# Hybrid decoder trunk: which 32-byte place the split weight tiles start at

## The chip, the cores and the metric

The kernel runs on one core of a Trainium2 chip. The metric is device time in microseconds (us). Two timed runs of the kernel before the change took 1570.54 and 1565.43 us; their median is 1567.99 us.

The engines named below are TensorE (PE in the profile, with PEld for its weight loads), VectorE (DVE), ScalarE (ACT), GpSimd (POOL) and SyncE (SP), which issues the transfers.

## The reference, cut to what matters

Two layers (`DEPTH = 2`) work on 256 tokens of width 1024. Each layer is a half-step SwiGLU feed-forward block, a mixer with a Mamba-2 and a gated DeltaNet branch, and a second feed-forward block:

```python
for l in range(DEPTH):
    h = h + 0.5 * swiglu(rms_norm(h, ffn1_norm[l]), ffn1_w_in[l], ffn1_w_out[l])
    u = rms_norm(h, mix_norm[l])
    (z_s, xbc, dt_s, qkv, z_d, b_d, a_d, gate_s, gate_d) = jnp.split(u @ w_in[l], split_points, axis=-1)
    y_s = mamba2_branch(...)
    y_d = deltanet_branch(...)
    merged = (jax.nn.sigmoid(gate_s) * (y_s @ ssm_w_branch[l])
              + jax.nn.sigmoid(gate_d) * (y_d @ dn_w_branch[l]))
    h = h + merged @ w_out[l]
    h = h + 0.5 * swiglu(rms_norm(h, ffn2_norm[l]), ffn2_w_in[l], ffn2_w_out[l])
return rms_norm(h, final_norm)
```

`swiglu(x, w_in, w_out)` is `(silu(gate) * up) @ w_out` with `gate, up = split(x @ w_in)`; its inner width is 2816. All data are float32. Nearly all of the arithmetic is in products of activations with weights that are read from memory once.

## The kernel before, in words

**Split weights.** A float32 product is made from float32r matmuls. A weight tile of 128 partitions x 1024 columns is split in two: `hi`, the float32r rounding of the weights, made by an ACT copy (the helper `act`, L66), and `lo`, the rest, made by a DVE subtraction (the helper `tt`, L69). Activations are split in the same way (`uT`, `gh` and `gl`, `bh` and `bl`, `mh` and `ml`), and a product is the sum of hi x hi, hi x lo and lo x hi.

**The stream of weights.** `plan` lists the 552 split tiles in the order of their use, and `stream` the transfers that they need. `load` issues a transfer of 512 KB on SP's queue into one of five `wraw` buffers (or, for the first tile of a group in the feed-forward blocks, into `wfirst`, which shares buffers with `yz`). `prep` makes `whi` and `wlo`, in five buffers each (`NSPL = 5`). `take` hands the next split tile to the matmuls, after running `load` and `prep` ahead for the tiles that follow. A few tiles (kinds `q0` to `q6`) are combined with others by DVE before or after they are split, for a Strassen-like scheme with fewer products in the second half of the feed-forward blocks.

**Who uses a split tile.** With the letters of the change (matmuls counted from the loops):

- `f` (16 tiles, 192 matmuls) and `t` (64 tiles, 768): `tok_chunk`, L287 to L289, tiles `f` and `t` of the profile. The weights are streamed, 512 columns a matmul; `uT` is the operand loaded beforehand (the stationary one).
- `c` (160 tiles): `chan_pair`, tile `fc`. Weights are loaded and `uT` is streamed: 1280 matmuls of 512 columns (L342, with `hi`) alternate with 1280 of 256 columns (L346, with `lo`).
- `h` (112 tiles, 2688 matmuls of 256 columns): `chan_chunk`, L292 to L294, tiles `kk`, `qq`, `vv`, `bc`, `zd` and `xs`, with weights loaded and `uT` streamed.
- `p` and `o` (112 and 24 tiles, 672 and 288 matmuls): the products with the feed-forward block's second matrix, in `block_products` and `out_chunks`. Weights are streamed, `gh`, `gl` or the block sums `bsa` to `bsd` are loaded.
- `b` (48 tiles, 576 matmuls) and `w` (16 tiles, 192): the mixer's branch products and its output product, in `out_chunks`. Weights are streamed, `bh` and `bl`, or `mh` and `ml`, are loaded.

That is 7936 matmuls in all.

**Order of the work.** The order is written out by hand: `FFN` is the order inside a feed-forward block, `ORDER` that of the mixer's units. Matmuls wait for their weights by semaphores; `issue_after` and `high_priority` place a few ACT and DVE steps.

**Addresses.** Tiles lie one behind the other in each partition, in the order of the pools `cpool`, `wpool`, `slots`, `s2`, `sm`; each starts at a multiple of 32 bytes. The text calls the start address modulo 128 bytes, divided by 32, the *place* of a tile, 0 to 3. In the program before, the addresses are: `h` 16512, `uT` 32928, `wraw` from 57984, `whi` from 78464, `wlo` from 98944, `slots` from 119424 (`gh` 123520, `gl` 148096, `bsa` 172672, `bsb` 178816), `s2` from 203392. A whole tile of weights is 4096 bytes = 32 x 128, so all ten split buffers start at place 0, as do `gh`, `gl`, the block sums, `bh`, `bl`, `mh` and `ml`. Alone among the matmul operands of split products, `uT` starts at place 1, because `mhalf` (4 bytes, rounded up to 32) lies ahead of it. Every slice that a matmul takes of these tiles begins a multiple of 512 bytes into the tile, and so has the tile's place.

Of the kernel before, what the change touches and what calls it, by code (L numbers as in the profile page):

```python
# [8 lines left out]
F32R = mybir.dt.float32r  # L9
I32 = mybir.dt.int32  # L10
AF = mybir.ActivationFunctionType
ALU = mybir.AluOpType
# [4 lines left out]
P = 128  # L17
D = 1024
S = 256
DEPTH = 2  # L20
# [9 lines left out]
NRAW = 5  # L30
NSPL = 5
START = 2

FFN = "f" + 8 * "c" + "A" + 4 * "c" + "A" + 4 * "c" + "A" + 2 * "c" + "A" + 2 * "c" + "BdBBBddddd"
# [7 lines left out]
ORDER = """  # L44
# [7 lines left out]
def trunk_kernel(ctx, tc, x, wst, wsm, norms, lpar, rpar, cst, out):  # L52
    nc = tc.nc
    V, A, G, PE = nc.vector, nc.scalar, nc.gpsimd, nc.tensor

    cpool = ctx.enter_context(tc.tile_pool(name="cpool", bufs=1))
    wpool = ctx.enter_context(tc.tile_pool(name="wpool", bufs=1))
# [7 lines left out]
    def act(o, i, func=AF.Copy, **kw):  # L65
        return A.activation(out=o, in_=i, func=func, **kw)  # L66

    def tt(o, a, b, op):
        return V.tensor_tensor(out=o, in0=a, in1=b, op=op)  # L69
# [9 lines left out]
    def f(ap):  # L79
        return ap.bitcast(F32)  # L80

    def tmp2(name):
        return s2.tile([P, 512], F32, tag="s2", name=name)
# [52 lines left out]
    n_forms = len(plan)  # L136
# [3 lines left out]
    def load(j):  # L140
# [5 lines left out]
        state["last"] = nc.sync.dma_start(r[:], wst[stream[j] // 2, :, (stream[j] % 2) * 1024 :][:, 0:1024])  # L146
        raws[j] = r

    def prep(i):
        kind, js, _ = plan[i]  # L150
        hi = wpool.tile([P, 1024], F32R, tag="whi", name="whi", bufs=NSPL)
        lo = wpool.tile([P, 1024], F32R, tag="wlo", name="wlo", bufs=NSPL)

        def less(o, a, b):
            tt(raws[js[o]][:], raws[js[a]][:], raws[js[b]][:], ALU.subtract)


        r = raws[js[{"q2": 1, "q4": 4, "q5": 3}.get(kind, 0)]]
        with ExitStack() as behind:
            for ins in state["behind"].pop(i, ()):  # L160
                behind.enter_context(tc.issue_after(ins))
            act(hi[:], r[:])
            if kind == "q1":
                less(1, 2, 1)
            elif kind == "q2":
                less(0, 2, 0)
            elif kind == "q4":
                less(0, 3, 0)
            tt(lo[:], r[:], f(hi[:]), ALU.subtract)
            if kind == "q0":  # L170
                less(0, 1, 0)
        for o in {"d": (0,), "q2": (1,), "q3": (2,), "q4": (4,), "q5": (3,), "q6": (0,)}.get(kind, ()):
            raws.pop(js[o])
        halves[i] = (hi, lo)

    def ahead(key, n, fn):
        while state[key] < n:
            fn(state[key])
            state[key] += 1

    def take():
        j = state["taken"]
        state["taken"] = j + 1
        ahead("loaded", min(plan[min(j + NSPL, n_forms) - 1][2] + NRAW - 1, n_raw), load)
        ahead("prepped", min(j + 1 if state["hold"] else j + NSPL, n_forms), prep)
        return halves.pop(j)
# [11 lines left out]
    h = cpool.tile([P, 2, D], F32, name="h")  # L198
# [34 lines left out]
    def rstd_of(t):  # L233

        ss = small([P, 2], "ss")
        for n in range(2):
            junk = tmp2("junk")
            state["square"] = act(junk[:], h[:, t, n * 512 : (n + 1) * 512], AF.Square, scale=1.0 / 32.0, accum_out=ss[:, n : n + 1])
        z = small([P, 2], "zz")
        ts(z[:, 0:1], ss[:, 0:1], ss[:, 1:2], ALU.add, EPS, ALU.add)  # L240
        rsqrt(z[:, 1:2], z[:, 0:1], [P, 1])
        return z[:, 1:2]
# [18 lines left out]
    def norm_in(nw, add=None):  # L261

        for t in range(2):
            with tc.high_priority(offset=PRI), ExitStack() as behind:
                if add:
                    add(t)
                    if t == 0:
                        behind.enter_context(tc.issue_after(state["sums"][5].ins))
                ins, done = rms_chain(t, nw)
            if t == 0:  # L270
                state["hold"] = False
                n = state["taken"]
                if not add:
                    ahead("prepped", n + 1, prep)
                    with tc.issue_after(done[0].ins), tc.issue_after(done[1].ins):
                        ahead("prepped", n + START, prep)
                with tc.issue_after(ins.ins):
                    ahead("prepped", n + 2, prep)
                if add:
                    state["behind"][n + 2] = [d.ins for d in done]  # L280
            elif add:

                state["behind"][n + 4] = (state["square"].ins, ins.ins)
                state["input"] = done
# [946 lines left out]
    for t in range(2):  # L1231
        add(t)
        o = [tmp2("fo") for _ in range(2)]
# [3 lines left out]
        r = rstd_of(t)  # L1237
# [137 lines left out]
```

## Time and profile before

| | before |
|---|---|
| timed runs | 1565.43 and 1570.54 us, median 1567.99 us |
| span of the profiled execution | 1565.8 us (no other time of it is recorded) |
| TensorE busy | 1545.0 us, 10152 matmuls |
| weight loads busy | 1342.0 us |
| DVE, ACT busy | 1302.4 us, 999.8 us |
| `fc` on L342, 512 columns | 1280, mean 391 ns |
| `fc` on L346, 256 columns | 1280, mean 282 ns |
| granted TensorE clock | 0.999 |

How to read it: a matmul's duration runs from its start to the end of its last result, and matmuls overlap, so the duration of 391 ns is not what a matmul costs. What it costs is the step from its start to the start of the next one, which the timeline shows. Where a group's mean duration is longer than that of another group of the same shape, its steps are as a rule longer too.

### The profile page before, as it was taken

Reading aid. Unit: us, or ns where it says so; the run is one execution under the profiler, and the core shown is the slowest. Engines: PE = TensorE matmul, PEld = TensorE weight load, DVE = VectorE, ACT = ScalarE, POOL = GpSimd, SP = SyncE. Lnnn points to the kernel's source line nnn. Section 1 sums busy time; section 2 is a strip of 40 time slices with the busy share of each in tenths; the row PEclk is TensorE's granted clock in tenths of the full one; section 3 lists DMA queues with packets and bytes.
Section 4 is the critical chain, followed back from the end, with each engine's and each line's share of the span. In section 5 each row is a group of like instructions: output and inputs, shape, how many; then the busy total and the mean of one; then the engine's idle time right before and its main releaser. Section 6 shows DMA issues by size and latency. Waiting matters only on the chain.

```text
span 1565.8 us, 26672 instructions
## 1 busy us (share of the span) xinstructions
PE 1545.0 (99%) x10152; PEld 1342.0 (86%) x10152; DVE 1302.4 (83%) x2048; ACT 999.8 (64%) x1694; POOL 53.2 (3%) x60
## 2 busy tenths in 40 slices
PE   8999999999999999999999999999999999999998
PEld 6888779999888888888788887899998888888886
DVE  6889969957899766899878998699579996679897
ACT  6666668766675655666566676686656666466664
POOL 0000010000000000000000001010000000000000
PEclk9999999999999999999999999999999999999999
DMA  8565565553455555465765566555336546555553
GB/s 298 197 214 188 195 212 173 178 158 118 174 207 173 177 205 196 159 210 177 262 204 187 168 198 223 189 189 189 116 123 213 177 166 212 201 175 166 198 189 134
DMA packets 94215, 292.99 MB, mean 187 GB/s; under 512 B 22325, under 2 KB 23301, under 8 KB 93062
## 3 DMA queue, kind: packets, MB, share of 16 engines
q1 hardware_dynamic: 94086, 291.29, 55.2%
q8 instruction: 79, 1.29, 0.3%
q14 instruction: 50, 0.41, 0.1%
HBM read 289.33 MB, written 1.92 MB: 186 GB/s over the span
## 4 chain that ended last, share of the span: by engine, by line
PE 76%; DVE 13%; DMA 5%; issue 3%; ACT 2%; POOL 1%; SPq 0%; POOLq 0%; DVEq 0%; ACTq 0%
PE fc L342 15%; PE fc L346 8%; DVE wlo L69 7%; PE t L287 3%; PE t L288 3%; PE t L289 3%; DMA wraw<-in_wst_dram 3%; PE b L289 3%; PE b L288 3%; PE b L287 2%; PE xs L292 2%; PE xs L293 2%; PE xs L294 2%; PE o L288 1%; PE o L289 1%
## 5 line engine op out<-in xcount | busy, mean ns | idle before, releaser
L69 DVE TENSOR_TENSOR wlo<-wraw,whi 128x1024 fp32r<-128x1024 f32 x488 | 591.0, 1221 | 139.8 <-ACT whi L66 136.1
L66 ACT ACTIVATE whi<-wraw 128x1024 fp32r<-128x1024 f32 x488 | 511.6, 1057 | 176.4 <-PE b L289 29.8
L342 PE MATMUL fc<-uT,whi 128*128 128x512 f32 x1280 | 445.5, 391 | 0.0
L346 PE MATMUL fc<-uT,wlo 128*128 128x256 f32 x1280 | 360.9, 282 | 0.0
L342 PEld LDWEIGHTS fc<-uT,whi 128*128 128x128 f32 x1280 | 240.3, 188 | 50.7
L346 PEld LDWEIGHTS fc<-uT,wlo 128*128 128x128 f32 x1280 | 241.8, 189 | 0.8
L287 PE MATMUL t<-whi,uT 128*128 128x512 f32 x256 | 102.9, 403 | 0.0
L288 PE MATMUL t<-wlo,uT 128*128 128x512 f32 x256 | 101.5, 396 | 0.2 <-DVE wlo L69 0.2
L289 PE MATMUL t<-whi,uT 128*128 128x512 f32 x256 | 101.5, 397 | 0.0
L66 ACT ACTIVATE whi<-wfirst 128x1024 fp32r<-128x1024 f32 x64 | 67.8, 1059 | 29.7 <-DVE wfirst L69 20.4
L66 ACT ACTIVATE sg<-fc 128x256 f32<-128x256 f32 x80 | 30.6, 382 | 82.3 <-PE fc L346 82.3
L69 DVE TENSOR_TENSOR wlo<-wfirst,whi 128x1024 fp32r<-128x1024 f32 x64 | 78.1, 1220 | 2.0 <-ACT whi L66 1.9
L287 PE MATMUL b<-whi,bh 128*128 128x512 f32 x192 | 76.1, 398 | 0.0
L288 PE MATMUL b<-wlo,bh 128*128 128x512 f32 x192 | 74.9, 390 | 0.0
L289 PE MATMUL b<-whi,bl 128*128 128x512 f32 x192 | 74.3, 394 | 0.3 <-DVE bl L69 0.3
L292 PE MATMUL xs<-uT,whi 128*128 128x256 f32 x256 | 73.1, 286 | 0.0
L294 PE MATMUL xs<-uT,wlo 128*128 128x256 f32 x256 | 71.6, 280 | 0.0
L293 PE MATMUL xs<-uT,whi 128*128 128x256 f32 x256 | 71.4, 279 | 0.0
L288 PE MATMUL o<-wlo,gh 128*128 128x512 f32 x160 | 64.6, 404 | 2.6 <-DVE wlo L69 2.5
L69 DVE TENSOR_TENSOR wfirst<-wraw,wfirst 128x1024 f32<-128x1024 f32 x48 | 58.6, 1220 | 8.9 <-DMA wraw<-in_wst_dram 8.9
L289 PE MATMUL o<-whi,gl 128*128 128x512 f32 x160 | 62.5, 391 | 0.0
L287 PE MATMUL o<-whi,gh 128*128 128x512 f32 x160 | 62.1, 392 | 0.0
(317 smaller groups left out, 3424.5 us busy)
## 6 DMA issues: line engine op xcount, KB each, us to landing
wraw<-in_wst_dram SPq DMA_DIRECT2D x504, 512.0 KB, 4.5
wfirst<-in_wst_dram SPq DMA_DIRECT2D x16, 512.0 KB, 5.8
dc<-rdram SPq DMA_DIRECT2D x8, 1024.0 KB, 8.4
nw<-in_norms_dram SPq DMA_DIRECT2D x6, 512.0 KB, 6.2
gb<-rdram SPq DMA_DIRECT2D x8, 256.0 KB, 5.3
h<-in_x_dram SPq DMA_DIRECT2D x4, 256.0 KB, 5.7
out_dram<-fo SPq DMA_DIRECT2D x4, 256.0 KB, 2.1
dq<-X SPq DMA_DIRECT2D x2, 256.0 KB, 5.0
```

What stands on the lines that cost most here:

```text
L66: return A.activation(out=o, in_=i, func=func, **kw)
L69: return V.tensor_tensor(out=o, in0=a, in1=b, op=op)
L287: PE.matmul(ps, lh, rh, start=start, stop=False)
L288: PE.matmul(ps, lh, rl, start=False, stop=False)
L289: return PE.matmul(ps, ll, rh, start=False, stop=stop)
L292: PE.matmul(ps, wh, mh, start=start, stop=False)
L293: PE.matmul(ps, wh, ml, start=False, stop=False)
L294: PE.matmul(ps, wl, mh, start=False, stop=stop)
L342: PE.matmul(ps[a][:], wh[:, c0 : c0 + P], uT[:, kt].rearrange("p o t -> p (o t)"), start=kt == 0, stop=False,)
L346: PE.matmul(ps[a][:, 0:S], wl[:, c0 : c0 + P], uTh[:, kt, :], start=False, stop=kt == KT - 1)
```

## The change

Each split buffer becomes 24 columns (96 bytes) longer, 1048 columns in place of 1024, so that the five buffers of a kind start at five addresses that step by 96 modulo 128. A tile then uses 1024 of these columns from an offset `skip` that puts its start at a chosen place. `BASE` holds the place of the first `whi` and `wlo` buffer in bytes, `turn` the buffer that the i-th tile gets. `uses` lists the kind of use of every tile, in order, and `places` chooses:

- `c` and `h`: `hi` at place n % 4 and `lo` at n // 4 % 4, n counting the units (two tiles each), so that 16 units run through all pairs;
- `f` and `t`: both parts at (n + 1) % 4, n counting groups of four tiles; `w`: the same with n counting tiles;
- `o`, `p` and `b`: both parts at place 0.

The ten longer buffers take 960 bytes more; the pools behind `wpool` start 960 bytes later. The instructions, their order, the transfers and the waits are those of before.

```diff
+BASE = (0, 96)
...
+    uses = []
+    for _ in range(DEPTH):
+        for sub in range(2):
+            for kind in FFN:
+                uses += {"f": "ffff", "c": "cc", "A": "pppp", "B": "ppp", "d": "o"}[kind]
+            if sub == 0:
+                uses += 4 * "t"
+                for name in ORDER:
+                    uses += {"z": "tt", "g": "tt", "N": 8 * "b"}.get(name[0], "hh" if name[0] in "kqvdbx" and len(name) > 1 else "")
+                uses += 16 * "b" + 8 * "w"
+    assert len(uses) == n_forms, (len(uses), n_forms)
+    nth = [uses[:i].count(u) for i, u in enumerate(uses)]
+    turn = [0, 4, 3, 2, 1]
+
+    def places(i):
+        u, n = uses[i], nth[i]
+        if u in "fh":
+            n //= 2 if u == "h" else 4
+        elif u == "c":
+            n //= 2
+        elif u == "t":
+            n //= 4
+        if u in "ch":
+            return n % 4, n // 4 % 4
+        if u in "ftw":
+            return (n + 1) % 4, (n + 1) % 4
+        return 0, 0
+
+    def split_tile(i, o, tag):
+        r = places(i)[o]
+        j = (turn[i % 5], turn[i % 5])[o]
+        base = (BASE[o] + 96 * j) % 128
+        skip = (32 * r - base) % 128 // 4
+        return wpool.tile([P, 1024 + 24], F32R, tag=tag, name=tag, bufs=NSPL)[:, skip : skip + 1024]
+
     def prep(i):
         kind, js, _ = plan[i]
-        hi = wpool.tile([P, 1024], F32R, tag="whi", name="whi", bufs=NSPL)
-        lo = wpool.tile([P, 1024], F32R, tag="wlo", name="wlo", bufs=NSPL)
+        hi = split_tile(i, 0, "whi")
+        lo = split_tile(i, 1, "wlo")
...
-            act(hi[:], r[:])
+            act(hi, r[:])
...
-            tt(lo[:], r[:], f(hi[:]), ALU.subtract)
+            tt(lo, r[:], f(hi), ALU.subtract)
```

## The prediction

> **What bounds the kernel now.** I read the busy totals first, then the chain of work that ended last, then that chain in single stretches, and last the start times of single matmuls.
>
> ```profile
> span 1565.8 us, 26672 instructions
> PE 1545.0 (99%) x10152; PEld 1342.0 (86%) x10152; DVE 1302.4 (83%) x2048; ACT 999.8 (64%) x1694; POOL 53.2 (3%) x60
> ...
> PE 76%; DVE 13%; DMA 5%; issue 3%; ACT 2%; POOL 1%; SPq 0%; POOLq 0%; DVEq 0%; ACTq 0%
> ```
>
> TensorE is busy 99% of the span and carries 76% of the chain. DVE, which makes the low parts, carries 13%, and weight transfers 5%. The clock is not in play: the granted share was 0.999.
>
> ```profile
> core 0: 1565.8 us, clock 0.999
> ```
>
> Where in the kernel do the 76% and the 13% lie? Two stretches of the chain show it, one among the token units of the mixer and one at the end of a feed-forward block.
>
> ```profile
> by line: PE t L287 24.9%; PE t L289 24.9%; PE t L288 24.8%; PE ydb L1059 10.9%; PE yob L1065 3.5%; PE xsb L1045 2.9%; PE xs L293 2.7%; PE xs L292 2.7%; PE xs L294 2.7%
> ...
> by line: DVE wlo L69 32.8%; DMA wraw<-in_wst_dram 21.5%; issue 15.4%; DVE wfirst L69 5.0%; PE o L288 4.0%; PE o L289 3.2%; DVE g L69 3.0%; PE o L287 2.8%; DVE u L72 2.4%; DVE h L72 2.1%; DVE hn L72 1.6%; ACT junk L66 1.5%; DVE gl L69 1.4%;
> ```
>
> From 500 to 530 us every piece is TensorE: there a nanosecond per matmul is a nanosecond of the end. From 140 to 190 us the chain runs over DVE and the transfers, so a slower matmul there costs little. The other three feed-forward blocks have the same kind of stretch, and these rows count their `o` and then their `p` matmuls:
>
> ```profile
> 140.00:190.00 50.00, 31.40 (x132) 24.32 (x132) 1.38 (x2) 0.00 (x0) 1.00 0.62 210
> 734.00:784.00 50.00, 32.07 (x133) 24.20 (x133) 1.38 (x2) 0.00 (x0) 1.00 0.75 252
> 914.00:966.00 52.00, 31.65 (x134) 24.64 (x135) 1.38 (x2) 0.00 (x0) 1.00 0.59 202
> 1504.00:1552.00 48.00, 26.65 (x114) 21.09 (x115) 0.69 (x1) 0.00 (x0) 1.00 0.53 176
> ...
> 140.00:190.00 50.00, 5.62 (x24) 4.44 (x24) 3.42 (x5) 0.59 (x1) 1.00 0.62 210
> 734.00:784.00 50.00, 5.17 (x23) 3.94 (x21) 3.42 (x5) 0.59 (x1) 1.00 0.75 252
> 914.00:966.00 52.00, 5.62 (x24) 4.44 (x24) 3.41 (x5) 0.59 (x1) 1.00 0.59 202
> 1504.00:1552.00 48.00, 5.62 (x24) 4.44 (x24) 3.42 (x5) 0.59 (x1) 1.00 0.53 176
> ```
>
> That is 513 + 95 = 608 matmuls that I take as covered by DVE and the transfers.
>
> **What the change does to the work.** It adds and removes no instruction, no wait and no DMA, and moves no step in any queue. Only addresses change. So every cost must show as a different duration of the same instruction, and three kinds use the moved tiles: the ACT copy that writes `whi`, the DVE subtraction that writes `wlo`, and the matmuls that read both.
>
> *The writers.* `uT` lies at place 1 already, every other big tile at place 0:
>
> ```profile
> L69 DVE TENSOR_TENSOR gl<-g,gh 128x512 fp32r<-128x512 f32 x40 | 27.5, 687 | 0.0
> L69 DVE TENSOR_TENSOR uT<-hnT,uT 128x512 fp32r<-128x512 f32 x24 | 15.4, 682 | 0.0
> L66 ACT ACTIVATE uT<-hnT 128x512 fp32r<-128x512 f32 x24 | 13.7, 596 | 14.2 <-PE hnT L254 13.8
> L66 ACT ACTIVATE yz<-t 128x512 f32<-128x512 f32 x16 | 9.3, 594 | 4.4 <-PE t L289 4.3
> ```
>
> DVE writes place 1 in 682 ns and place 0 in 687, ACT in 596 and 594. I cost the writers at nothing, and with them the DVE work in the covered stretches; their own rows, which must then stay as they are, are these:
>
> ```profile
> L69 DVE TENSOR_TENSOR wlo<-wraw,whi 128x1024 fp32r<-128x1024 f32 x488 | 591.0, 1221 | 139.8 <-ACT whi L66 136.1 <-PE ksb L898 0.3
> L66 ACT ACTIVATE whi<-wraw 128x1024 fp32r<-128x1024 f32 x488 | 511.6, 1057 | 176.4 <-PE b L289 29.8 <-PE xs L293 24.2 <-PE fc L342 20.1
> ```
>
> *The transfers.* `wraw` lies ahead of the enlarged tiles and keeps its address. The 16 `wfirst` loads and the mixer's row loads land 64 bytes further on. No row bounds that from both sides; I take nothing, since the chain's 5% is named for `wraw`.
>
> *The matmuls.* Weights of the next matmul are loaded while the present one streams, so two operands are read at a time. Let r be the place of the streamed operand minus that of the loaded one, modulo 4. Four pairs of rows give the step from one matmul to the next, as the difference of the first and last start over the count:
>
> ```profile
> 98.27 0.39 PE L287 MATMUL p<-whi,bsb 128*128 128x512 f32 x1
> 102.12 0.39 PE L289 MATMUL p<-whi,bsb 128*128 128x512 f32 x1
> ...
> 229.25 0.40 PE L287 MATMUL t<-whi,uT 128*128 128x512 f32 x1
> 232.52 0.40 PE L289 MATMUL t<-whi,uT 128*128 128x512 f32 x1
> ...
> 105.14 0.39 PE L342 MATMUL fc<-uT,whi 128*128 128x512 f32 x1
> 111.73 0.39 PE L342 MATMUL fc<-uT,whi 128*128 128x512 f32 x1
> ...
> 239.82 0.28 PE L292 MATMUL kk<-uT,whi 128*128 128x256 f32 x1
> 244.72 0.28 PE L292 MATMUL kk<-uT,whi 128*128 128x256 f32 x1
> ```
>
> - `p`, r = 0 (both at place 0): 17 steps in 3.85 us, **226.5 ns**.
> - `t`, r = 3 (weights streamed from 0, `uT` loaded from 1): 14 steps in 3.27 us, **233.6 ns**.
> - `fc`, r = 1 (`uT` streamed, weights loaded): 19 pairs of a 512- and a 256-column matmul in 6.59 us, 346.8 ns a pair.
> - `kk`, r = 1, 256 columns: 42 steps in 4.90 us, **116.7 ns**. That leaves 346.8 - 116.7 = **230.1 ns** for the 512-column matmul at r = 1.
>
> Same shape, same clock, 7.1 ns between r = 0 and r = 3: this is the disputed quantity. The Trainium skill, "TensorE: Matmul & The Clock Gate", section "Part 2: What happens when you issue a matmul", says that TensorE has two independent SBUF read ports and that loading the next weights takes no read bandwidth from the running matmul; by it the places would not matter and the sum would be zero. The row of `t` speaks against it, but only `t` and `f` do.
>
> r = 2 occurs nowhere in the trace. The steps rise 226.5, 230.1, ?, 233.6, so I put it between its neighbours, at (230.1 + 233.6) / 2 = 231.9; the ends I keep are 226.5 below (as good as r = 0) and 237.2 above (r = 3 and half of the known spread of 7.1 again; an estimate). The mean of the four is 230.5.
>
> Now the units, with matmuls counted from the code:
>
> 1. `f` and `t`, 192 + 768 = 960: weights streamed at place (n+1) % 4 against `uT` at 1, so r runs 0, 1, 2, 3 from one group of four tiles to the next. 960 x (230.5 - 233.6) = **-3.0 us**.
> 2. `o`, `p`, `b`, 288 + 672 + 576 = 1536: their weights stay at place 0, but the ten enlarged buffers add 10 x 96 = 960 = 7 x 128 + 64 bytes ahead of all later pools, which puts `gh`, `gl`, the block sums, `bh` and `bl` at place 2. r goes from 0 to 2. Less the 608 covered: 928 x (231.9 - 226.5) = **+5.0 us**, from nothing to 928 x (237.2 - 226.5) = +9.9 by the ends kept.
> 3. `w`, 192: rotates against operands now at place 2: 192 x (230.5 - 226.5) = **+0.8 us**.
> 4. 512-column matmuls of `c`, 1280: r from a constant 1 to all four in turn: 1280 x (230.5 - 230.1) = **+0.5 us**.
> 5. 256-column ones, 1280 of `c` and 2688 of the channel units: only r = 1 is measured. Taking the same differences, 3968 x 0.4 = **+1.6 us**. Bounds: with r = 0 at the rate per column of `p`, 226.5 / 2 = 113.2, and all others as now, 3968 / 4 x (113.2 - 116.7) = -3.5 us; with three places in four 7.1 ns dearer, +21 us.
>
> Sum -3.0 + 5.0 + 0.8 + 0.5 + 1.6 = **+4.9 us**. The profile gives the span, 1565.8 us, and no time around it; the two timed runs shown lie 0.4 below and 4.7 above it, their median 2.2 above. On the median 1567.99 the forecast is **1573 us**. A measurement of this kernel can tell about 2%, 31.4 us, from no change, and this is a sixth of that.
>
> **Rivals.**
>
> - *Two places apart is quiet.* If r = 2 costs as r = 0, item 2 is zero; item 1 has the mean (226.5 + 230.1 + 226.5 + 233.6) / 4 = 229.2, so -4.2; item 3 +0.5; item 4 -1.2; item 5 with 113.2 in half the units and 116.7 and 120.2 in the others has a mean 0.9 lower, -3.5. Sum -8.4: **1560 us**. For it: operands two places apart have most room between them. Against: r = 0, no room at all, is the best row there is.
> - *The place is no cause.* The 7.1 ns belong to the token units for another reason, and no address matters: **1568 us**. For it: only units on `uT` show the extra time. Against: `p` streams from the same weight buffers at the same clock.
> - *Every load that starts off place 0 costs, whatever is streamed.* `t` loads `uT` from place 1 and pays 7.1 ns; `fc` and `kk` load from 0. After the change the 1536 + 192 - 608 = 1120 loads of `o`, `p`, `b`, `w` sit at place 2, and three in four of 2560 + 2688 loads of weights, 3936, off place 0, while `f` and `t` stay as they are. (1120 + 3936) x 7.1 = +35.9 us: **1604 us**, slower by over 2%. It decides from 31.4 / 5056 = 6.2 ns a load. For it: it fits all four rows as well. Against: it asks that a stream from place 1 costs nothing, while `kk`, which streams from place 1, takes 116.7 / 256 = 0.456 ns a column and `p`, from place 0, 226.5 / 512 = 0.442.
> - *The places don't hold.* If the buffer of the i-th tile is not the one that `turn` says, places drift within a unit; all four relations still occur evenly, so within 3 us of the forecast, **1573 us**, with unlike steps inside one unit.
>
> **How the numbers follow.** Forecast 0.40, two apart quiet 0.26, no cause 0.15, off place 0 dear 0.13, places drifting 0.06. Faster by over 2% needs -31 us, which no case gives: 0.02, for an r = 2 far below 226.5. Slower by over 2% is the third rival in most of its span: 0.10. Within 2%: 0.88. The range runs from 1554, the first rival less twice the 2.6 us by which the timed runs lie off their median, to 1595, which is 1573 with item 5 at its upper bound (+21 for +1.6) and 2.6 us of scatter, and leaves out the full price of the third rival.
>
> **What would show it.** Right: `t` units that step by 226 to 234 ns, each unit alike in itself and every fourth one near 226.5; `p` on the block sums at about 232 instead of 226.5; `whi` and `wlo` still written in about 1057 and 1221 ns; the chain's shares unchanged within two points. Wrong: `p` still at 226.5 (first or second rival), `kk`-like units up by 7 ns in three of four (third rival), writers whose mean moved, or a `wfirst` that lands later and shows on the chain. The forecast fails most easily in r = 2, which no row shows, and in the 256-column units, half of all split matmuls, where one relation of four is measured.

## The result and the profile after

The changed kernel took 1579.7 and 1578.3 us, median 1579.0 us, against 1567.99 us before: a ratio of 1.007, 95% interval 1.0049 to 1.0091, or 11 us more (7.7 to 14.3). The profiled execution took 1579.7 us, 1.8 us more than its span. The forecast was 1573 us, range 1554 to 1595.

From the page of the changed kernel, the span, the busy times and the chain by engine:

```profile
span 1577.9 us, 26672 instructions
...
PE 1557.0 (99%) x10152; PEld 1344.6 (85%) x10152; DVE 1303.4 (83%) x2048; ACT 1001.6 (63%) x1694; POOL 53.3 (3%) x60
...
PE 83%; DVE 8%; DMA 4%; issue 2%; ACT 2%; POOL 0%; SPq 0%; POOLq 0%; ACTq 0%; DVEq 0%
```

The span grew by 12.1 us and the busy time of TensorE by 12.0, with the same 10152 matmuls; DVE and ACT grew by 1.0 and 1.8. The writers of the split tiles have the means that they had (groups by line; the numbers behind the bar are busy us and mean ns of one):

```profile
L70 DVE TENSOR_TENSOR wlo<-wraw,whi 128x1024 fp32r<-128x1024 f32 x488 | 590.8, 1221 | 145.2 <-ACT whi L67 142.9 <-PE ksb L934 0.4
L67 ACT ACTIVATE whi<-wraw 128x1024 fp32r<-128x1024 f32 x488 | 512.6, 1057 | 181.1 <-PE b L325 30.8 <-PE xs L329 25.4 <-PE fc L378 20.5
```

The timeline of the changed kernel shows where the 12 us are: in the steps between matmuls. First `p` on the block sums, six rows and the last of the same run of matmuls, then the first and last 512-column matmul of one `fc` unit (high and low both at place 1):

```profile
99.92 0.40 PE L323 MATMUL p<-whi,bsb 128*128 128x512 f32 x1
100.16 0.40 PE L324 MATMUL p<-wlo,bsb 128*128 128x512 f32 x1
100.39 0.39 PE L325 MATMUL p<-whi,bsb 128*128 128x512 f32 x1
100.62 0.39 PE L323 MATMUL p<-whi,bsb 128*128 128x512 f32 x1
100.86 0.39 PE L324 MATMUL p<-wlo,bsb 128*128 128x512 f32 x1
101.08 0.39 PE L325 MATMUL p<-whi,bsb 128*128 128x512 f32 x1
...
103.84 0.40 PE L325 MATMUL p<-whi,bsb 128*128 128x512 f32 x1
...
53.80 0.40 PE L378 MATMUL fc<-uT,whi 128*128 128x512 f32 x1
59.07 0.40 PE L378 MATMUL fc<-uT,whi 128*128 128x512 f32 x1
```

`p`: 17 steps in 3.92 us, 230.6 ns, where it was 226.5, and the steps are no longer alike (0.24, 0.23, 0.23, 0.24, 0.22 us in these rows). `fc`: 15 pairs in 5.27 us, 351.3 ns, where it was 346.8.

The next table gives each kind's mean step over the whole trace, from the start of each matmul to that of the next; steps over 245 ns (512 columns) or 135 ns (256 columns) hold a wait and are left out of the mean. "Sum" is the difference times the count. `o` contains `w`, which writes a tile of the same name, and the `p` products that share its banks, so the counts by tile differ from those by letter; `channel` is the six tiles of the `h` units.

| steps, ns | count | before | after | sum, us |
|---|---|---|---|---|
| `f`, `t` | 960 | 233.1 | 232.2 | -0.8 |
| `p`, `o` (with `w`), `b` | 1728 | 227.7 | 231.4 | +6.4 |
| `fc`, 512 columns | 1280 | 228.6 | 231.8 | +4.0 |
| `fc`, 256 columns | 1280 | 118.3 | 117.9 | -0.5 |
| channel, 256 columns | 2688 | 116.8 | 118.2 | +3.7 |

Together +12.8 us, for 12.1 us of span; the difference lies in the steps left out of the means and in the other 2216 matmuls. Two single profiles fix the total no better than this, because waits differ between executions: in the layout with room and all tiles at 0 (below), whose steps are those of before, the profiled span was 2.4 us longer than that of the kernel before.

### The profile page after: what moved, and what is told of

It reads as the page before. It is cut to its first block, busy times and chain, and to the rows that moved or that the text cites. A ratio compares the mean times of both kernels' runs of the same rounds, so it can differ in the third digit from the quotient of the medians.

```text
span 1577.9 us, 26672 instructions
## 1 busy us (share of the span) xinstructions
PE 1557.0 (99%) x10152; PEld 1344.6 (85%) x10152; DVE 1303.4 (83%) x2048; ACT 1001.6 (63%) x1694; POOL 53.3 (3%) x60
## 4 chain that ended last, share of the span: by engine, by line
PE 83%; DVE 8%; DMA 4%; issue 2%; ACT 2%; POOL 0%; SPq 0%; POOLq 0%; ACTq 0%; DVEq 0%
PE fc L378 18%; PE fc L382 9%; DVE wlo L70 5%; PE t L324 3%; PE t L323 3%; PE t L325 3%; DMA wraw<-in_wst_dram 3%; PE b L325 3%; PE b L323 3%; PE b L324 3%; PE xs L329 2%; PE xs L328 2%; PE p L323 2%; PE p L325 2%; PE xs L330 2%
## 5 line engine op out<-in xcount | busy, mean ns | idle before, releaser
L70 DVE TENSOR_TENSOR wlo<-wraw,whi 128x1024 fp32r<-128x1024 f32 x488 | 590.8, 1221 | 145.2 <-ACT whi L67 142.9
L67 ACT ACTIVATE whi<-wraw 128x1024 fp32r<-128x1024 f32 x488 | 512.6, 1057 | 181.1 <-PE b L325 30.8
```

## The experiments

Three theories stood against each other. *Relation*: the forecast's own, in which the cost of a matmul is set by the place of the streamed operand less that of the loaded one, modulo 128 bytes. *Rhythm*: steps are short and repeat as long as one relation of addresses repeats from matmul to matmul, and become uneven and longer where it changes between high and low or from tile to tile. *Off place*: any load away from place 0 costs. All ratios are against the kernel before, run beside it on the same chip; mean steps are worked out as in the table above.

**Later pools alone.** The split buffers of before, and 960 bytes of nothing ahead of the later pools:

```diff
+    gap = ctx.enter_context(tc.tile_pool(name="gap", bufs=1))
     slots = ctx.enter_context(tc.tile_pool(name="slots", bufs=1))
+    gap.tile([P, 240], F32, name="gap")
```

> Only the 960 bytes behind the weight pool: split buffers as before, all later pools 64 bytes past place 0. Relation theory (the cost of a matmul is set by the place of the streamed operand less that of the loaded one, modulo 128 bytes): r goes from 0 to 2 for the 1728 matmuls of o, p, b and w, step 226.5 to about 231.9, with 608 of them covered +6 us on the kernel before. Rhythm theory (steps are short and even as long as one relation of addresses repeats from matmul to matmul, and uneven and longer where it changes): one relation still repeats, so p keeps one even step, whichever, and the broken pattern of steps between 225 and 239 ns that the changed kernel shows in p is gone; time within 3 us of before. Off-place theory (any load away from place 0 costs 7.1 ns): +8 us.

1572.82 us, ratio 1.0015 (1.0003 to 1.0027). First and last of a run of 18 `p` matmuls:

```profile
98.61 0.39 PE L289 MATMUL p<-whi,bsb 128*128 128x512 f32 x1
...
102.50 0.40 PE L291 MATMUL p<-whi,bsb 128*128 128x512 f32 x1
```

17 steps in 3.89 us, 228.8 ns; single steps repeat 226, 229, 232 ns. So two places apart costs about 2 ns a matmul where weights are streamed and nothing else changes, not the 5.4 of the forecast, and the pattern is a regular one. The off-place theory (+8 us) is out: the interval ends at 4.2 us.

**All tiles at place 0.** The change with `r = 0` in `split_tile`, and 64 bytes more ahead of the later pools, so that no place differs from before:

```diff
-        r = places(i)[o]
+        r = 0
...
+    gap.tile([P, 16], F32, name="gap")
```

> The changed kernel's longer buffers, but every split tile put at place 0, and 64 bytes more behind the pool so that the later pools lie at place 0 too: every place modulo 128 is as before, only the distances beyond 128 bytes differ from buffer to buffer and between high and low. Relation theory: nothing changes, 0 us against before, p at 226.5, fc pairs at 346.8. Rhythm theory with a period above 128 bytes: the relation changes from tile to tile as in the changed kernel, p near 231.7, fc pairs near 350, channel units near 118, +8 to +12 us.

1576.57 us, ratio 1.0049 (1.0034 to 1.0064). Groups of `p` on the first of the block sums, in the kernel before and in this one:

```profile
L287 PE MATMUL p<-whi,bsa 128*128 128x512 f32 x48 | 18.7, 389 | 0.0
```

```profile
L325 PE MATMUL p<-whi,bsa 128*128 128x512 f32 x48 | 18.9, 393 | 0.0
```

No place modulo 128 bytes changed, and yet 7.7 us are lost: `p`, `o`, `b` step by 230.8 ns in place of 227.7 (+5.5 us), `fc` pairs +1.9 us, channel units +2.1. The relation modulo 128 is therefore not the whole cause. What is new here lies beyond 128 bytes: worked out from the addresses, the tiles now start at two addresses modulo 256, 128 bytes apart, in turn, and in one buffer of five the low part has the other address than its high part. In this trace the `fc` tiles of that buffer take 350.5 ns a pair and those of the other four 347.4 to 349.4, while in the kernel before all five take 347.0 or 347.1.

**`uT` moved alone**, by a pad of A bytes ahead of it and 512 - A behind it (A = 480, 96, 32, 64, 288), so that every other tile keeps its address modulo 512 and every relation repeats. The names tell how far `uT` then lies past the weights, modulo 512; before, it is 32.

```diff
+    cpool.tile([P, A // 4], F32, name="pada")
     uT = cpool.tile([P, KT, 2, S], F32R, name="uT")
+    cpool.tile([P, (512 - A) // 4], F32, name="padb")
```

> The kernel before with uT moved alone, to the same address modulo 512 bytes as the weights; all else keeps its address modulo 512. Relation theory: f and t go from r = 3 to r = 0, 960 x -7.1 = -6.8 us; the 512-column matmuls of c go from r = 1 to r = 0, 1280 x -3.6 = -4.6 us; the 256-column ones between 0 and 3968 x -3.5 = -13.9 us: between -11 and -25 us. Rhythm theory: one relation repeats everywhere, so all steps are even and t takes the step of p, 226.5: -6.3 us from t and f, channel units open. Off-place theory: -6.8 us from f and t, nothing else.

> As the run with uT at the same address modulo 512, but 128 bytes further on. If 128 bytes is the whole period, time and steps are those of that run within 1 us. If the period is longer, t or the channel units take another step than there.

> The kernel before with uT alone moved, to 64 bytes past the weights modulo 512, so that every product with uT has operands two places apart and all addresses still repeat. Rhythm theory: each kind of unit takes one even pattern; the few channel units of the changed kernel with both parts two places from uT that settled did so at 113.3 ns, so channel units 2688 x (113.3 - 116.8) = -9.4 us; t and f at the 229 ns that the run with the later pools moved shows for two places apart, 960 x -4 = -3.8 us; fc open, 343 to 352 ns a pair (-5 to +6 us): faster than before by 7 to 18 us. Relation theory of the forecast (r = 2 between its neighbours): 960 x (231.9 - 233.6) = -1.6, 1280 x 1.8 = +2.3, 3968 x 1.8 = +7: slower by 8 us.

> As the run with uT 64 bytes past the weights, but 256 bytes further on. If the pattern has a period of 256 bytes or less, the same steps and the same time within 1 us; if not, other steps in t, fc or the channel units, as 0 and 128 bytes gave different ones.

> uT 96 bytes past the weights: the last of the four places for products with uT, addresses repeating. Rhythm theory: even steps in every unit, of a length that no run shows yet, between 113 and 121 ns in the channel units. Relation theory: t and f at r = 1, 230.1, -3 us; the others at r = 3, 1280 x 3.5 + 3968 x 3.5 = +18 us.

| `uT` past the weights | time, us | ratio (interval) | `t` | `fc` pair | channel |
|---|---|---|---|---|---|
| 32 (before) | | 1 | 233.1 | 346.9 | 116.8 |
| 0 | 1581.05 | 1.0077 (1.006 to 1.0094) | 227.7 | 353.1 | 119.9 |
| 128 | 1579.01 | 1.0057 (1.004 to 1.0074) | 232.5 | 350.9 | 118.8 |
| 64 | 1576.86 | 1.0033 (1.0021 to 1.0046) | 233.3 | 350.5 | 117.3 |
| 320 | 1575.55 | 1.0032 (1.002 to 1.0044) | 233.3 | 349.8 | 117.1 |
| 96 | 1584.2 (one run) | | 234.1 | 350.2 | 119.9 |

With `uT` at relation 0 the token units take the step that `p` had before, and the channel units step by an even 120 ns. First and last of 13 `t` matmuls, then of 13 channel matmuls, in that run:

```profile
230.63 0.40 PE L291 MATMUL t<-whi,uT 128*128 128x512 f32 x1
...
233.36 0.39 PE L291 MATMUL t<-whi,uT 128*128 128x512 f32 x1
...
242.97 0.28 PE L294 MATMUL kk<-uT,whi 128*128 128x256 f32 x1
...
244.41 0.28 PE L294 MATMUL kk<-uT,whi 128*128 128x256 f32 x1
```

12 steps in 2.73 us are 227.5 ns; 12 in 1.44 us are 120.0. So relation 0, the cheapest of the six for streamed weights, is the dearest of them for `fc` with loaded weights: the price of a relation does not carry over from one kind of unit to the other. Both theories that were left had this run faster than before, by 6 us or more, and it was slower by 0.77%: even steps can be long ones. 0 and 128 bytes give different steps in all three kinds, so 128 bytes is not the period; 64 and 320 give the same within 1 ns a pair, so 256 bytes can be. And of the six, the distance of 32 bytes that the kernel before happens to have is the best for `fc` and channel units. My expectation for 64 (channel units at 113.3 ns, `t` at 229, the whole 7 to 18 us faster) was a miss: `t` stayed at 233.3, and of 224 stretches of 12 matmuls there, 25 settled at 113 to 114 ns and 198 at 116.5 or more, at the same addresses. What decides between the two states was not found.

**Low parts 64 bytes further, in every unit alike.** The low tiles in a pool of their own:

```diff
+    gapa = ctx.enter_context(tc.tile_pool(name="gapa", bufs=1))
+    gapa.tile([P, 16], F32, name="gapa")
+    lpool = ctx.enter_context(tc.tile_pool(name="lpool", bufs=1))
...
-        lo = wpool.tile([P, 1024], F32R, tag="wlo", name="wlo", bufs=NSPL)
+        lo = lpool.tile([P, 1024], F32R, tag="wlo", name="wlo", bufs=NSPL)
```

and 448 bytes of nothing behind that pool.

> The kernel before with all low parts 64 bytes past the high parts, modulo 512, and everything else in place: high and low two places apart, but the same in every unit and with nothing changing from unit to unit. If high and low apart is what breaks the even steps, p near 231 and channel units near 118 with uneven steps, +5 to +10 us. If only the change from tile to tile breaks them, even patterns that repeat every three matmuls, time between -3 and +5 us.

1579.73 us, ratio 1.006 (1.004 to 1.008): nearly as large a loss as that of the change, with nothing that changes from unit to unit. The first and last of 18 `p` matmuls:

```profile
99.61 0.40 PE L293 MATMUL p<-whi,bsb 128*128 128x512 f32 x1
...
103.55 0.39 PE L295 MATMUL p<-whi,bsb 128*128 128x512 f32 x1
```

17 steps in 3.94 us, 231.8 ns. Over the trace `p` goes from 227.3 to 232.4, `o` from 227.9 to 231.9, `b` from 228.1 to 231.9, together +7.2 us; `fc` pairs and the channel units add 3.3 and 2.6. High and low at different addresses are enough to break the short steps where weights are streamed against `gh`, `bh` and the like; `f` and `t`, on `uT`, stay at 233.0.

**A layout with room.** Buffers of 4352 bytes, 17 x 256, so that a tile can be put at any of the four places and all buffers still agree modulo 256. The code below is set against the changed kernel. To make room, the tile `one` went to a slot and `rows` to the `s2` pool.

```diff
-        j = (turn[i % 5], turn[i % 5])[o]
-        base = (BASE[o] + 96 * j) % 128
-        skip = (32 * r - base) % 128 // 4
-        return wpool.tile([P, 1024 + 24], ...)[:, skip : skip + 1024]
+        skip = 8 * r
+        return wpool.tile([P, 1024 + 64], ...)[:, skip : skip + 1024]
```

Four versions of `places`: all at 0; `f` and `t` at place 1 and the rest at 0; the places of the change with the high part's place for both parts; and the places of the change as they are.

> Every split buffer 256 bytes longer than a tile, and nothing shifted: all operands keep their addresses modulo 256 bytes, as in the kernel before, while modulo 512 the buffers alternate between 128 and 384. (To make room, the one-row tile of ones lies in a slot and the 1 KB tile of scalar rows in a buffer of the s2 pool.) Rhythm theory with a period of 256 bytes: even steps as before, p 226.7, fc pairs 347, time within 2 us of before. If the pattern needs 512 bytes: uneven steps and +5 to +8 us, as with all places 0.

> The 256-byte layout, with the tiles of f and t alone moved by 32 bytes, high and low together, so that they have the same address modulo 256 as uT; c and the channel units keep uT 32 bytes past their weights, o, p, b and w stay. Both theories: f and t take the 227.6 ns that they had with uT moved to relation 0, 960 x (227.6 - 233.1) = -5.3 us, and nothing else moves: 4 to 6 us faster than before, a little less if changes of place between units cost some uneven steps.

> The 256-byte layout with places that change from unit to unit as in the change, but high and low always at the same place, and later pools at place 0. Each unit should be even in itself. From the runs with uT moved (0, 32, 64, 96 bytes past the weights: fc pairs 353.1, 346.9, 350.5, 350.2; channel units 119.9, 116.8, 117.3, 119.9; t 227.7, 233.1, 233.3, 234.1), their means against before: 1280 x 3.3 + 2688 x 1.7 - 960 x 1.0 = +4.2 + 4.5 - 1.0 = +8 us. If only high and low apart costs, and change from unit to unit does not: 0.

> The same 256-byte layout with the places of the change as they are, high and low apart in fc and channel units, later pools at place 0: the change without its uneven distances beyond 128 bytes and without the 64 bytes of the later pools. o, p and b back at 226.7: -5 us against the changed kernel. fc and the channel units stay uneven at about 350 a pair and 118: +7 us against before. If the distances beyond 128 bytes were the whole cost, 0.

| | time, us | ratio (interval) | `f`, `t` | `p`, `o`, `b` | `fc` pair | channel |
|---|---|---|---|---|---|---|
| all at 0 | 1569.97 | 0.9994 (0.9985 to 1.0002) | 233.2 | 227.8 | 346.9 | 116.8 |
| `f`, `t` at 1 | 1567.37 | 0.9979 (0.9969 to 0.9989) | 227.9 | 227.8 | 346.9 | 116.8 |
| rotating, high = low | 1575.19 | 1.0029 (1.0019 to 1.0039) | 231.0 | 228.3 | 351.6 | 117.6 |
| rotating, apart | 1573.98 | 1.0025 (1.0013 to 1.0036) | 231.0 | 228.4 | 349.3 | 118.0 |

The first row settles the period: modulo 512 the buffers alternate, modulo 256 they agree, and neither the time nor any step differs from before. The same `p` group as above, in this run:

```profile
L308 PE MATMUL p<-whi,bsa 128*128 128x512 f32 x48 | 18.7, 389 | 0.0
```

The third row prices the rotation itself. Two neighbouring `fc` units of that run, first and last 512-column matmul of each, the first unit at place 0 and the second at place 1:

```profile
48.17 0.39 PE L374 MATMUL fc<-uT,whi 128*128 128x512 f32 x1
...
53.37 0.39 PE L374 MATMUL fc<-uT,whi 128*128 128x512 f32 x1
...
53.72 0.40 PE L374 MATMUL fc<-uT,whi 128*128 128x512 f32 x1
...
59.02 0.40 PE L374 MATMUL fc<-uT,whi 128*128 128x512 f32 x1
```

15 pairs in 5.20 us are 346.7 ns; 15 in 5.30 are 353.3. The means over all 20 units of each place are 347.6, 352.9, 353.5 and 352.6: three places in four cost 5 to 6 ns a pair. The mean of the run is 351.6 against 346.9 before, over 1280 pairs 6.0 us. Keeping high and low together did not help `fc`; apart, the pair is cheaper by 2.3 ns on average and the channel units dearer by 0.4, and the two ratios overlap. Both runs lost less than I had expected (8 and 7 us): 4.6 and 3.9 us.

**A version faster than both.** The second row is faster than the kernel before by 0.21% (0.11 to 0.31%), 3.3 us, and so also than the changed one. Its `t` group, and that of the row above it, as the mean of one:

```profile
L308 PE MATMUL t<-whi,uT 128*128 128x512 f32 x256 | 101.8, 399 | 0.0
```

```profile
L308 PE MATMUL t<-whi,uT 128*128 128x512 f32 x256 | 103.0, 403 | 0.0
```

Only `f` and `t` moved, by 32 bytes, high and low together: 960 x (227.9 - 233.2) = -5.1 us of steps, of which 3.3 reach the end. The Trainium skill, "TensorE: Matmul & The Clock Gate", section "Part 2: What happens when you issue a matmul", says that loading the next weights takes no SBUF read bandwidth from the running matmul. In this trace 32 bytes between the loaded and the streamed operand make 5 ns a matmul, so the step is not free of the loaded operand's address, and the measurement decides; whether bandwidth is what the 5 ns are, no run shows.

Moving the weights gave `f` and `t` 227.9 ns, and moving `uT` to the same relation 227.7. So the difference of the two addresses counts, not the address of either.

## Why the prediction was right or wrong

**The result.** It was slower by less than 2%, as forecast, and lies in the range. But the sum of +4.9 us became +12.8 us of steps and 11 us of time, because several of its terms were wrong. That the time lies in the range is in part luck: the upper end stood at 1595 because item 5 could have cost 21 us, and item 5 took 3.2; of what came on top, item 4 made 3.5 us and item 1 made 2.2, and the range held no room for either.

**Item 1, `f` and `t`: -3.0 forecast, -0.8 measured.** The direction was right. With even buffers the four relations cost 227.8, 233.3, 229.7 and 233.0 ns (rotating, high = low), mean 231.0, close to the 230.5 of the forecast; in the changed kernel they cost 230.7, 233.3, 231.6 and 233.1. The cheap relations lost 2 to 3 ns where high and low, or one tile and the next, lie at different addresses modulo 256. The sign that I named, every fourth group near 226.5, did not come.

**Items 2 and 3, `o`, `p`, `b` and `w`: +5.8 forecast, +6.4 of steps measured.** The forecast counted only what the end would see, and the 6.4 are all steps. The step of `p` was forecast at about 232 and is 231.7. That is a right number from a wrong step. Interpolated as the price of r = 2, it is too high: the run with the later pools alone has 229.3 as the mean of the three kinds, +2.7 us. The rest goes with the uneven distances, which the forecast did not count at all: the run with all places 0 loses 5.5 us in these kinds without any change of place.

**The cover of the 608.** In the first block the `o` matmuls look covered. From the first `o` matmul of the closing stretch to the first `t` matmul behind it, in the kernel before:

```profile
157.69 0.39 PE L287 MATMUL o<-whi,bsc 128*128 128x512 f32 x1
...
193.06 0.39 PE L287 MATMUL t<-whi,uT 128*128 128x512 f32 x1
```

and in the changed one:

```profile
159.99 0.39 PE L323 MATMUL o<-whi,bsc 128*128 128x512 f32 x1
...
195.32 0.39 PE L323 MATMUL t<-whi,uT 128*128 128x512 f32 x1
```

35.37 and 35.33 us, although the 144 `o` matmuls in it step by 3.7 ns more, 0.5 us. In the same block's stretches before that, by the starts of the first `p` of each group, 0.2 to 0.3 us were added each time, so the `p` matmuls there were hardly covered. The other three closing stretches of 144 `o` matmuls changed by +0.4, -0.4 and +2.0 us. These differences neither prove the cover nor refute it, since they scatter by more than the 0.5 us: in the layout with room and all tiles at 0 the four stretches differ from before by +0.3, -1.1, +0.9 and +1.6 us with steps that are those of before.

**Item 4, `fc` with 512 columns: +0.5 forecast, +4.0 measured; with the 256-column half, +3.5.** This is the term that failed most. I took the 512-column price at r = 1 as the difference of two rows, 230.1, and then the mean over four places from units that stream weights, 230.5. The one is 228.6 by direct steps, and the other does not hold where `uT` is streamed: there the distance of 32 bytes is the cheapest by 3 to 6 ns a pair in the table of `uT` moved alone. Leaving it in three units of four is what costs in the rotating run with high = low. In the changed kernel the uneven distances come on top: units with the high part at place 0 take 349.2 ns a pair, the others 349.3 to 350.2. How its 3.5 us divide between the two is open.

**Item 5, 256 columns: +1.6 forecast, +3.2 measured** (+3.7 channel, -0.5 `fc`). Inside the bounds of -3.5 and +21; 120 ns, the highest that any place shows, is 3.2 above the step of before.

**The writers** at nothing: right, 1057 and 1221 ns.

**The rivals.** "Two places apart is quiet" is out: with `uT` 64 bytes past the weights, `t` stays at 233.3 and `fc` pairs rise to 350.5. "The place is no cause" is out: moving `uT` alone takes `t` from 233.1 to 227.7. "Off place 0 is dear" is out by the run with the later pools. "The places don't hold" was nearest to what happened, in a way that I had not thought of: the places held modulo 128 bytes, and modulo 256 they did not. No trace holds an address, but the token units bear out the places: in the changed kernel the five groups at place 1 step by 230.3 to 231.2 ns, at place 3 by 230.8 to 232.0, at 0 and 2 by 232.5 to 233.6, and with all places 0 every group lies at 232.7 to 234.0.

**A sign that misled.** I had said that the chain's shares would stay within two points; TensorE went from 76% to 83%. This says nothing of the change: the layout with room and all tiles at 0 has the time of the kernel before and a chain with 82%.

```profile
PE 82%; DVE 9%; DMA 4%; issue 2%; ACT 2%; POOL 1%; SPq 0%; POOLq 0%; DVEq 0%; ACTq 0%
```

**How the 11 us divide** is only partly settled. Alone, the later pools cost 0.15%, the uneven distances 0.49%, the rotation with high and low apart 0.25%. They add up to 0.89%, which the intervals don't tell from the 0.7% of the whole. The steps show that they don't simply add: in `p`, `o` and `b` the three make 2.7, 5.5 and 1.2 us, against 6.4 in the changed kernel, and in `fc` the last two make 1.9 and 3.1, against 3.5.

## What to carry to other kernels

When a kernel is bound by back-to-back matmuls, compare the steps between starts, not the durations, of groups with the same shape: a few nanoseconds there can be addresses. Padding a buffer moves more than the operand it is meant for: it changes the distance between all buffers of the ring and the place of every later pool. Here 96 bytes a buffer cost 0.49% by themselves and 256 bytes nothing, so pad by a multiple of 256 bytes and test the padding alone. A price measured in one kind of unit (weights streamed) is no estimate for another (weights loaded).

## What the runs showed of the hardware that was not expected

- The step of a float32r matmul depended on the address of the streamed operand less that of the loaded one, modulo 256 bytes: for 512 streamed weight columns 227.7 ns at 0, 229.3 at 64, 232.5 at 128, and 233 to 234 at 32, 160, 192 and 224. Distances that differed by 256 gave the same steps within 1 ns a pair; 0 and 128, and 64 and 192, did not. With the weights loaded and `uT` streamed the order was another: a pair took 346.9 ns at 32 and 353.1 at 0.
- With one relation that repeats, the steps settled into a fixed pattern within about five matmuls after a wait: 227, 227, 226 ns, or 226, 229, 232, or an even 120. With high and low 64 bytes apart, 224 to 241 ns in no order that I could name, and a higher mean, 232.
- At the same addresses two patterns can exist: channel units with `uT` 64 bytes past the weights ran at 113 ns in 25 stretches of 224 and at 116.5 or more in 198.
- What in the chip makes these steps, and why 256 bytes, no run here shows.
